# Two decoder layers on one core: the plain up-weight tile split first and kept in a slot, two more landing buffers, six staggered gate tiles ahead of the pairs, a later sample-state update

## The chip, the core and the metric

The kernel runs on one core of one Trainium2 chip. The metric is the device time of one execution in microseconds (us); lower is better. The engines are named as the profile names them: PE (TensorE, matmuls), DVE (VectorE), ACT (ScalarE), POOL (GpSimd), SP (SyncE, which issues the DMAs here). Each engine works through its own list of instructions in order; an instruction that has to wait holds up all that stand behind it on the same engine.

## What is computed

1024 prompt positions and 8 sample positions (together W = 1032 columns) go through two decoder layers with shared weights, width 1024, FFN width 2816:

```python
def swiglu(hn, w_gate_up, w_down):
    gu = hn @ w_gate_up
    return (jax.nn.silu(gu[..., :D_FF]) * gu[..., D_FF:]) @ w_down

def run_trunk(...):
    for layer in range(DEPTH):                      # DEPTH = 2
        hn = rmsnorm(x, norm_mix[layer])
        out = mixer_ab(hn, ...) if layer % 2 == 0 else mixer_c(hn, ...)
        x = x + out                                 # residual after the output projection
        x = x + swiglu(rmsnorm(x, norm_ffn[layer]), w_gate_up[layer], w_down[layer])
    y = rmsnorm(x, norm_final)
```

Layer 0 mixes by a gated DeltaNet (4 heads, each with a 128 x 128 state per sample) and an RG-LRU; layer 1 by sliding-window attention. The outputs are the activations and all states. `co_sample` computes the sample part of the DeltaNet, and its second half writes the new states: for each of the 8 parts of the states an outer product (one matmul of 512 columns) is added to the decayed old state.

## The kernel before

**Numbers in pieces.** Every fp32 weight tile is split into a high part `wh` (cast on ACT) and a low part `wl` (difference on DVE); activations are split the same way. A product is then three matmuls per 128 rows of contraction: wh·xh, wh·xl, wl·xh.

**Gate and up by seven products.** For each of the KF = 22 feature tiles f, gate and up weights (A11, A12 for gate, A21, A22 for up, each half of the contraction) and the two halves of the columns (B11, B21 and B12, B22) are multiplied in Winograd's form of Strassen's scheme. Seven products of 4 x 3 matmul groups stand for eight: A11·B11, A12·B21, S1·T1, S2·T2, S3·T3, S4·B22 and A22·T4. S1 to S4 are sums of weight tiles that POOL makes (`Pair.sums`, four operations); T1 to T4 are sums and differences of activation tiles that `co_blocks` makes on DVE and POOL, in four steps k = 0 to 3, each of which also makes the k-th quarter of T2 and B22; T1, T3 and T4 are split after the four steps. The evacuations of the products (`plus`) are DVE's, those of A11·B11 and A12·B21 ACT's.

**Ahead of the pairs.** T2 needs the normalised activations of both column halves, A11·B11 and A12·B21 only those of the first. So `run_gu` computes these two products of the first AHEAD = 4 tiles before anything else, one tile after the other (`first(f)`, then `second(f, a)`). The second product adds to the bank that ACT has copied out after the first, so it waits for that copy. Then come the pairs: those four tiles with five products each (S2, S1, S3, S4, A22), the other 18 with seven.

**Weights on their way.** SP loads a raw tile of 512 KB into one of two landing buffers (`raw`); it is split into a ring of WB = 4 pairs `wh`, `wl`; a buffer is loaded again when all of its readers are done (`read`, `load_raw`). `split_next` takes the next weight unit of the list `units`; it is called twice after every product, and a unit can be split only when the unit four places before it has been used up. In a pair the unit A22 is last, so the up tile's buffer stays taken until then.

**What sets the order.** The program is written out by a scheduler (`Sched`) with its own cost model: main products are emitted in order, and the generators (`co_blocks`, `co_sample`, `co_h`, ...) are woken between matmuls when the model's clock says that their inputs are ready. What each engine gets is a fixed list. Intermediate tiles live in SLOTS = 40 slots of one buffer, which `alloc` and `halloc` (half a slot) hand out.

**The sample-state update** (second half of `co_sample`) may start when `in1` (the input projection) is done and more than 4 slots are free.

## Time and profile before

| | us |
|---|---|
| median of 3 runs (lowest, highest) | 2420.78 (2417.97, 2423.76) |
| the profiled execution's own time | 2415.7 |
| its span, first to last instruction | 2413.7 |
| PE busy (share of the span) | 2291.8 (95%) |
| DVE, ACT, POOL busy | 1323.1, 990.9, 808.4 |
| mean granted clock of PE | 0.981 of full speed |

The page gives for each engine its busy share in 40 equal slices of 60 us. PE stands at 9 (over 90%) nearly everywhere; the slices that do not are where the FFN of a layer begins: from about 540 to 660 us (the tenth and eleventh slice) for layer 0, and from about 1690 to 1750 us (the 29th) for layer 1. A time in a row of the timeline is counted from the span's start; "[4.77 <-ACT s L235]" means that the engine sat idle for 4.77 us before that row and that ACT, writing a tile s, ended it. All instructions bear the line of the helper that records them (L235), so rows are told apart by engine, tile name and shape: `wh`, `wl` are split weights, `raw` a landing buffer, `s` a slot, `PS` a PSUM bank.

### The profile page before, as it was taken

Reading aid. Unit: us, or ns where it says so; the run is one execution under the profiler, and the core shown is the slowest. Engines: PE = TensorE matmul, PEld = TensorE weight load, DVE = VectorE, ACT = ScalarE, POOL = GpSimd, SP = SyncE. Lnnn points to the kernel's source line nnn. Section 1 sums busy time; section 2 is a strip of 40 time slices with the busy share of each in tenths; the row PEclk is TensorE's granted clock in tenths of the full one; section 3 lists DMA queues with packets and bytes.
Section 4 is the critical chain, followed back from the end, with each engine's and each line's share of the span. In section 5 each row is a group of like instructions: output and inputs, shape, how many; then the busy total and the mean of one; then the engine's idle time right before and its main releaser. Section 6 shows DMA issues by size and latency. Waiting matters only on the chain.

```text
span 2413.7 us, 40193 instructions
## 1 busy us (share of the span) xinstructions
PE 2291.8 (95%) x15984; PEld 2119.8 (88%) x15984; DVE 1323.1 (55%) x2295; ACT 990.9 (41%) x2015; POOL 808.4 (33%) x738
## 2 busy tenths in 40 slices
PE   9899999997699999999999999999799999999998
PEld 6779988786599999999999789778699999999998
DVE  7888586575644444462336557556654444462324
ACT  6676765533222222241214677654322222241214
POOL 1534363243444444410002444432454444420003
PEclk9999999998699999999999999999899999999999
DMA  4342123254122222263213211334122222262312
GB/s 156 105 126 80 40 91 102 77 166 121 49 82 83 81 82 76 79 239 100 102 51 109 77 56 56 128 118 141 53 81 78 80 79 79 80 246 91 99 53 84
DMA packets 114747, 233.90 MB, mean 97 GB/s; under 512 B 23728, under 2 KB 50144, under 8 KB 114528
## 3 DMA queue, kind: packets, MB, share of 16 engines
q1 hardware_dynamic: 114272, 231.05, 29.9%
q8 instruction: 126, 2.06, 0.4%
q14 instruction: 61, 0.50, 0.1%
q10 hardware_dynamic: 288, 0.29, 0.0%
HBM read 187.72 MB, written 45.66 MB: 97 GB/s over the span
## 4 chain that ended last, share of the span: by engine, by line
PE 77%; DVE 10%; ACT 5%; issue 4%; POOL 2%; DMA 1%; SPq 0%; DVEq 0%; ACTq 0%; POOLq 0%
PE PS L235 77%; DVE s L235 7%; ACT s L235 3%; DVE wl L235 2%; POOL s L235 2%; ACT wh L235 1%; DVE oss L235 0%; SPq L235 0%; DMA s<-ckT 0%; ACT L235 0%; DMA raw<-wgu 0%; DMA hd<-s 0%; DMA s<-xT 0%; ACT mx L235 0%; DMA raw<-wout 0%
## 5 line engine op out<-in xcount | busy, mean ns | idle before, releaser
L235 PE MATMUL PS<-s,wh 128*128 128x260 f32 (+3 forms) x8640 | 1724.2, 316 | 69.5 <-ACT s L235 39.7
L235 PEld LDWEIGHTS PS<-s,wh 128*128 128x128 f32 x8640 | 1326.3, 190 | 154.2 <-ACT s L235 51.7
L235 PE MATMUL PS<-s,wl 128*128 128x260 f32 (+3 forms) x4320 | 1045.7, 314 | 0.0
L235 PEld LDWEIGHTS PS<-s,wl 128*128 128x128 f32 x4320 | 714.9, 190 | 33.2 <-issue 0.9
L235 POOL TENSOR_TENSOR s<-s,s 128x520 f32<-128x520 f32 (+6 forms) x214 | 305.7, 1430 | 781.3 <-ACT s L235 702.6
L235 DVE TENSOR_TENSOR wl<-raw,wh 128x512 fp32r<-128x512 f32 (+1 forms) x403 | 342.6, 855 | 382.9 <-ACT wh L235 382.4
L235 DVE TENSOR_TENSOR s<-PS,s 128x520 f32<-128x520 f32 (+7 forms) x430 | 293.5, 683 | 381.7 <-PE PS L235 302.4
L235 ACT CAST wh<-raw 128x512 fp32r<-128x512 f32 (+1 forms) x428 | 257.5, 608 | 385.5 <-PE PS L235 365.8
L235 POOL TENSOR_TENSOR s<-raw 128x512 f32<-128x512 f32 x88 | 115.1, 1308 | 383.6 <-DMA raw<-wgu 383.6
L235 DVE TENSOR_TENSOR wl<-s,wh 128x512 fp32r<-128x512 f32 x176 | 150.3, 855 | 168.8 <-ACT wh L235 148.0
L235 ACT CAST wh<-s 128x512 fp32r<-128x512 f32 x176 | 108.7, 620 | 298.8 <-POOL s L235 220.9
L235 PE MATMUL PS<-s,s 64*64 64x64 f32 (+11 forms) x1936 | 210.0, 288 | 12.8 <-DVE s L235 7.0
L235 PEld LDWEIGHTS PS<-s,s 128*128 128x128 f32 (+3 forms) x1936 | 171.9, 158 | 47.9 <-issue 15.6
L235 ACT ACTIVATE s<-s 128x520 f32<-128x520 f32 (+5 forms) x197 | 123.4, 632 | 194.1 <-DVE s L235 172.6
L235 ACT COPY s<-PS 128x512 f32<-128x512 f32 (+6 forms) x296 | 129.6, 468 | 170.9 <-PE PS L235 162.1
L235 DVE TENSOR_TENSOR s<-s,s 128x520 fp32r<-128x520 f32 (+8 forms) x186 | 168.9, 934 | 40.7 <-ACT s L235 38.7
L235 ACT CAST s<-s 128x520 fp32r<-128x520 f32 (+4 forms) x200 | 138.7, 711 | 103.5 <-DVE s L235 48.2
L235 DVE SCALAR_TENSOR_TENSOR s<-s,smt,s 128x512 f32<-128x512 f32 (+3 forms) x151 | 121.6, 832 | 13.9 <-ACT s L235 13.4
L235 PE MATMUL PS<-con,s 128*128 128x128 f32 (+2 forms) x659 | 91.3, 271 | 26.1 <-ACT s L235 15.5
L235 PEld LDWEIGHTS PS<-con,s 128*128 128x128 f32 (+1 forms) x659 | 77.0, 155 | 37.8 <-ACT s L235 17.0
L235 POOL TENSOR_SCALAR s<-s,mx 128x256 f32<-128x256 f32 x64 | 64.5, 1020 | 108.4 <-ACT s L235 71.8
L235 POOL TENSOR_TENSOR s<-s,con 64x256 f32<-64x256 f32 (+1 forms) x56 | 59.4, 1062 | 64.7 <-ACT s L235 30.2
(176 smaller groups left out, 1038.2 us busy)
## 6 DMA issues: line engine op xcount, KB each, us to landing
raw<-wgu SPq DMA_DIRECT2D x96, 512.0 KB, 3.6
raw<-win SPq DMA_DIRECT2D x47, 512.0 KB, 3.6
s<-hd SPq DMA_DIRECT2D x44, 516.0 KB, 6.0
raw<-wout SPq DMA_DIRECT2D x32, 512.0 KB, 3.5
raw<-wdn SPq DMA_DIRECT2D x24, 512.0 KB, 3.7
raw<-wqkv SPq DMA_DIRECT2D x24, 512.0 KB, 3.5
hd<-s SPq DMA_DIRECT2D x44, 260.0 KB, 4.4
hd<-s SPq DMA_DIRECT2D x44, 256.0 KB, 3.3
```

Source lines behind the costliest of these rows:

```text
L235: return sched.call(eng, op, lambda: f(*a, **kw), a, kw)
```

## The change

1. AHEAD goes from 4 to 6, and the twelve early products are staggered: the first product of tile f+1 stands between the first and the second of tile f. Each early tile's two results share one slot (`twins`).
2. RAW_MORE = 2: when the first column half of the output projection is done, two slots become further landing buffers (`more_raws`); they are given back in the early loop.
3. In each pair the unit A22 is split first, into a slot of its own and outside the ring, so that the sums and this split free the up tile's buffer at once. It asks for three free slots, unless a product already needs it (`force`).
4. The sample-state update waits for `steady` (the fourth pair of layer 0) as well as `in1`, with more than 2 free slots. `co_blocks` takes its sums in pairs of halves.

```diff
-AHEAD = 4
+AHEAD = 6
+RAW_MORE = 2
+    def twins():
+        wait_free()
+        t, i = new_slot(F32)
+        owner[i] = 0
+        return [Buf(t[:, HW * h:HW * (h + 1)], i, h, F32) for h in range(2)]
...
     def read(raw):
         raw.left -= 1
-        while rpos[0] < len(raws) and raws[rpos[0] - 2].left == 0:
+        if raw.left == 0:
+            h = raw.home
+            if isinstance(h, str) or more[0]:
+                homes.append(h)
+            else:
+                free(h)
+        while rpos[0] < len(raws) and homes:
             load_raw()
+    def more_raws(n):
+        more[0] = n
+        if n:
+            homes.extend(alloc() for _ in range(n))
+            while rpos[0] < len(raws) and homes:
+                load_raw()
...
-        if u >= WB and units[u - WB].left and not units[u - WB].keep:
+        x = units[u]
+        r = x.r - x.slot
+        if r >= WB and ring_units[r - WB].left:
             return
...
+        elif x.slot:
+            if len(free_slots) < 3 and not force:
+                return
+            x.buf = alloc(F32R)
...
-            yield have("in1")
-            yield lambda: len(free_slots) > 4
+            yield have("in1", "steady")
+            yield lambda: len(free_slots) > 2
...
-                self.units(("S2", "S1", "S3", "S4", "A22") if f < AHEAD else
-                           ("A11", "S2", "A12", "S1", "S3", "S4", "A22"), layer)
+                self.units(("A22", "S2", "S1", "S3", "S4") if f < AHEAD else
+                           ("A22", "A11", "S2", "A12", "S1", "S3", "S4"), layer)
...
-                for f in range(AHEAD):
-                    a, p = first(f)
-                    kept_[f] = p, second(f, a)
+                pend = None
+                for f in range(AHEAD + 1):
+                    pg = twins() if f < AHEAD else None
+                    new = first(f, pg[0]) + (pg[1],) if f < AHEAD else None
+                    if f:
+                        kept_[f - 1] = pend[1], second(f - 1, pend[0], pend[2])
+                    pend = new
+                    if f == AHEAD - 3:
+                        more_raws(0)
                 for f in range(KF):
+                    if f == 3:
+                        ready.add("steady")
```

How the lists move is shown at three places. SP, start of the FFN of layer 0, before; `raw` is loaded from `wgu`, and `o_pgc` to `o_s_lru` are small outputs:

```order
L235 DMA raw_5789<-wgu 128x1024
L235 DMA o_pgc<-PGC_101 128x36
...
L235 DMA o_s_gdn<-s18_612 128x4x128
L235 DMA s18_612<-s_gdn_in 128x4x128
L235 DMA raw_5866<-wgu 128x1024
L235 DMA raw_5915<-wgu 128x1024
L235 DMA raw_5940<-wgu 128x1024
```

The same place now (`raw0`, `raw1`, `s33`, `s34` are the four landing buffers):

```order
L236 DMA s33_5197<-wgu 128x1024
L236 DMA s16_5085<-xT 128x520
L236 DMA xe06_118<-s2_4993 128x520
L236 DMA s34_5198<-wgu 128x1024
L236 DMA xe07_119<-s16_5085 128x520
L236 DMA o_pgc<-PGC_101 128x36
...
L236 DMA raw1_5823<-wgu 128x1024
L236 DMA raw0_5881<-wgu 128x1024
L236 DMA s33_5197<-wgu 128x1024
```

In the first list raw_5866 and raw_5915 are gate and up of pair 0, right behind four early tiles; in the second the last three rows are early tile 5 and then gate and up of pair 0, with five early tiles ahead of them and no state loads between. DVE, layer 0, before, from the last early split to the middle of step k = 1 of `co_blocks` (the rows with smt are its scaled activations; the row with con is the sample update):

```order
L235 TENSOR_TENSOR wl_5912<-raw_5789,wh_5911 128x512
L235 TENSOR_TENSOR wl_5933<-s17_5934,wh_5932 128x512
L235 TENSOR_TENSOR wl_5958<-s1_5929,wh_5957 128x512
L235 TENSOR_TENSOR wl_5976<-s17_5934,wh_5975 128x512
L235 TENSOR_TENSOR s21_5106<-s15_3580,con_73 128x512
L235 TENSOR_TENSOR wl_5999<-s16_5935,wh_5998 128x512
L235 TENSOR_TENSOR s23_789<-PS_72,s23_789 128x512
L235 SCALAR_TENSOR_TENSOR s6_4364<-s6_4364,smt_74,s37_1537 128x520
L235 SCALAR_TENSOR_TENSOR s9_4900<-s9_4900,smt_74,s37_1537 128x520
```

DVE, layer 0, now, from the splits between steps 0 and 1 to the splits between steps 1 and 2:

```order
L236 TENSOR_TENSOR wl_5878<-raw0_5583,wh_5877 128x512
L236 TENSOR_TENSOR wl_5899<-s34_5198,wh_5898 128x512
L236 TENSOR_TENSOR wl_5920<-s33_5197,wh_5919 128x512
L236 TENSOR_TENSOR wl_5940<-raw1_5823,wh_5939 128x512
L236 SCALAR_TENSOR_TENSOR s7_4324<-s7_4324,smt_74,s12_5801 128x520
L236 SCALAR_TENSOR_TENSOR s11_4868<-s11_4868,smt_74,s12_5801 128x520
...
L236 TENSOR_TENSOR wl_5967<-s34_5198,wh_5966 128x512
L236 TENSOR_TENSOR wl_5987<-raw1_5823,wh_5986 128x512
L236 TENSOR_TENSOR s13_5992<-s33_5197,s13_5992 128x512
L236 TENSOR_TENSOR wl_6017<-s30_5993,wh_6016 128x512
L236 TENSOR_TENSOR wl_6040<-s30_5993,wh_6039 128x512
```

Before, all four splits of S sums (rows wl from an s) stand ahead of step 1; now step 1 stands ahead of them, between early splits, and then come A22 (s13) and two S splits. PE, the sample update's matmul (s with s, 512 columns) before, within the first product of pair 0, S2·T2:

```order
L235 MATMUL PS_72<-s27_5898,wh_5932 128x260 x4
L235 MATMUL PS_72<-s27_5898,wl_5933 128x260 x2
L235 MATMUL PS_72<-s21_5106,s15_3580 128x512
L235 MATMUL PS_72<-s31_6018,wh_5932 128x260 x4
L235 MATMUL PS_72<-s31_6018,wl_5933 128x260 x2
```

PE now, where the first of these matmuls stands, in the product S4·B22 of pair 3:

```order
L236 MATMUL PS_72<-s35_5910,wh_6586 128x260 x4
L236 MATMUL PS_72<-s35_5910,wl_6587 128x260 x2
L236 MATMUL PS_72<-s17_6029,wh_6586 128x260 x3
L236 MATMUL PS_72<-s15_3610 128x512
L236 MATMUL PS_72<-s17_6029,wh_6586 128x260
```

Before, three of the eight stood in the output projection, one in the first early product and four in pair 0; now all eight stand in pairs 3 to 7.

## Rows read from the trace of the kernel before

**Rows 1.** The page's 40 slices: busy tenths of PE in each.

```profile
PE   9899999997699999999999999999799999999998
```

**Rows 2.** Stretches: busy us (and instructions) by engine, granted clock, DMA share, GB/s.

```profile
558.20:650.80 92.60, 58.50 (x248) 46.84 (x247) 56.49 (x69) 26.94 (x49) 35.88 (x34) 0.72 0.24 70
650.80:690.00 39.20, 34.60 (x280) 33.67 (x280) 18.59 (x24) 8.15 (x14) 18.64 (x13) 1.00 0.28 82
1670.50:1739.20 68.70, 49.23 (x243) 40.47 (x242) 45.29 (x55) 25.68 (x47) 30.05 (x30) 0.85 0.20 62
1739.20:1800.00 60.80, 57.22 (x447) 55.27 (x446) 29.03 (x38) 14.75 (x25) 27.18 (x20) 1.00 0.27 88
```

**Rows 3.** Waits of PE from 558.2 to 650.8: total us, times, longest.

```profile
PE PS L235 <- ACT s L235: 21.2, 9, 5.0
PE PS L235 <- DVE s L235: 11.6, 10, 2.4
```

**Rows 4.** Timeline of PE, layer 0: start, us, instruction, [idle before].

```profile
557.83 0.40 PE L235 MATMUL PS<-s,wl 128*128 128x260 f32 x2
...
574.16 0.73 PE L235 MATMUL PS<-s,wh 128*128 128x512 f32 x2 [0.67 <-ACT s L235]
...
591.28 1.22 PE L235 MATMUL PS<-s,wh 128*128 128x512 f32 x2 [4.77 <-ACT s L235]
...
602.54 0.80 PE L235 MATMUL PS<-s,wh 128*128 128x260 f32 x2 [5.03 <-ACT s L235]
...
623.42 0.80 PE L235 MATMUL PS<-s,wh 128*128 128x260 f32 x2 [1.33 <-DVE wl L235]
...
650.35 0.61 PE L235 MATMUL PS<-s,wl 128*128 128x260 f32 x2
```

**Rows 5.** Timeline of SP's queue, layer 0.

```profile
573.28 17.68 SPq L235 DMA_DIRECT2D raw<-wgu  x3
```

**Rows 6.** Timeline of POOL, layer 0: the first sum of pair 0.

```profile
585.08 1.29 POOL L235 TENSOR_TENSOR s<-raw 128x512 f32<-128x512 f32 x1 [6.61 <-DMA raw<-wgu]
```

**Rows 7.** Timeline of ACT, layer 0: the first split of a sum.

```profile
587.75 0.62 ACT L235 CAST wh<-s 128x512 fp32r<-128x512 f32 x1 [7.13 <-POOL s L235]
```

**Rows 8.** Timeline of DVE, layer 0.

```profile
578.79 1.30 DVE L235 TENSOR_TENSOR s<-s,s 128x520 fp32r<-128x520 f32 x2 [0.69 <-ACT s L235]
...
588.40 2.76 DVE L235 TENSOR_TENSOR wl<-s,wh 128x512 fp32r<-128x512 f32 x2 [7.70 <-ACT wh L235]
...
592.78 1.78 DVE L235 TENSOR_TENSOR s<-s,con 128x512 fp32r<-128x512 f32 x1
...
602.52 3.14 DVE L235 TENSOR_TENSOR s<-s,s 128x520 fp32r<-128x520 f32 x2 [0.69 <-ACT s L235]
```

**Rows 9.** Timeline of PE, layer 1.

```profile
1670.17 0.40 PE L235 MATMUL PS<-s,wl 128*128 128x260 f32 x2
...
1672.77 2.29 PE L235 MATMUL PS<-con,s 128*128 128x1 f32 x20
...
1679.03 0.62 PE L235 MATMUL PS<-s,wh 128*128 128x512 f32 x2
...
1679.72 0.62 PE L235 MATMUL PS<-s,wh 128*128 128x512 f32 x2
...
1731.54 0.64 PE L235 MATMUL PS<-s,wh 128*128 128x260 f32 x4
...
1734.41 0.64 PE L235 MATMUL PS<-s,wh 128*128 128x260 f32 x4
...
1738.92 0.40 PE L235 MATMUL PS<-s,wl 128*128 128x260 f32 x2
```

**Rows 10.** Timeline of DVE, layer 1: scaled activations of steps 2 and 3, then six differences.

```profile
1704.88 1.42 DVE L235 SCALAR_TENSOR_TENSOR s<-s,smt,s 128x520 f32<-128x520 f32 x2
...
1712.06 1.42 DVE L235 SCALAR_TENSOR_TENSOR s<-s,smt,s 128x520 f32<-128x520 f32 x2
...
1719.67 5.88 DVE L235 TENSOR_TENSOR s<-s,s 128x520 fp32r<-128x520 f32 x6
```

More of the change, by code (lines that the diff above doesn't have):

```diff
@@ L454, in __init__ @@
         def __init__(self, wap, nk):
-            self.wap, self.nk, self.left, self.tile = wap, nk, 0, None
+            self.wap, self.nk, self.left, self.tile, self.home = wap, nk, 0, None, None
             raws.append(self)
     class Unit:
-        def __init__(self, key, src, n, left, raw=None, keep=False, before=None, after=None):
+        def __init__(self, key, src, n, left, raw=None, keep=False, before=None, after=None, slot=False):
             self.key, self.src, self.n, self.left, self.raw = key, src, n, left, raw
             self.keep, self.before, self.after = keep, before, after
+            self.slot, self.buf, self.r = slot, None, len(ring_units)
+            if not keep and not slot:
+                ring_units.append(self)
             if raw is not None:
@@ L486, in raw_dma @@
         SP.dma_start(out=raws[i].tile[:, a:b], in_=raws[i].wap[:, a:b])
+    homes = ["raw0", "raw1"]
+    more = [0]
     def load_raw(dma=True):
@@ L490, in load_raw @@
         rpos[0] += 1
-        raws[i].tile = ring_tile(wpool, "raw", 2, [128, 8, 128], F32)
+        h = raws[i].home = homes.pop(0)
+        raws[i].tile = ring_tile(wpool, h, 1, [128, 8, 128], F32) if isinstance(h, str) else \
+            h.a[:, 0:1024].rearrange("p (k c) -> p k c", k=8)
         if dma:
@@ L496, in read, with split_next @@
         raw.left -= 1
-        while rpos[0] < len(raws) and raws[rpos[0] - 2].left == 0:
-            load_raw()
-    def split_next():
+        if raw.left == 0:
[5 more added lines that the diff above has]
+        while rpos[0] < len(raws) and homes:
+            load_raw()
+    def more_raws(n):
[4 more added lines that the diff above has]
+                load_raw()
+        else:
+            for h in [h for h in homes if not isinstance(h, str)]:
+                homes.remove(h)
+                free(h)
+    def split_next(force=False):
         u = upos[0]
@@ L512, in split_next @@
             h, l = (kept[-1].a[:, 512 * i:512 * i + 512].rearrange("p (k c) -> p k c", k=4) for i in range(2))
+        elif x.slot:
+            if len(free_slots) < 3 and not force:
+                return
+            x.buf = alloc(F32R)
+            h, l = (x.buf.a[:, 512 * i:512 * i + 512].rearrange("p (k c) -> p k c", k=4) for i in range(2))
         else:
@@ L1514, in co_blocks @@
                 x1a, x2a = half(k, 0), half(4 + k, 0)
-                ls = [halloc() for _ in range(4)]
+                if k % 2 == 0:
+                    l13 = [twins() for _ in range(3)]
+                ls = [l13[0][k % 2], halloc(), l13[1][k % 2], l13[2][k % 2]]
                 l1, l2, l3, l4 = (b.a[:, 0:520] for b in ls)
@@ L1551, in __init__ @@
                     self.g = Raw(wgu[layer, f], 8)
-                    self.units(("A11", "A12"), layer)
                     return
@@ L1566, in units @@
                         raw, o = self.u if name == "A22" else self.g, 0 if name == "A11" else 4
-                        Unit(key, lambda raw=raw, o=o: raw.tile[:, o:o + 4], 4, 1, raw, before=first)
+                        Unit(key, lambda raw=raw, o=o: raw.tile[:, o:o + 4], 4, 1, raw, before=first,
+                             slot=name == "A22")
                     else:
@@ L1589, in ffn @@
             hd = [dpool.tile([128, W], F32, tag=f"hd{layer}{f}", name=f"hd{layer}{f}", bufs=1) for f in range(KF)]
-            for f in range(AHEAD):
-                Pair(layer, f, True)
+            firsts = [Pair(layer, f, True) for f in range(AHEAD)]
+            for f in range(AHEAD + 1):
+                if f < AHEAD:
+                    firsts[f].units(("A11",), layer)
+                if f:
+                    firsts[f - 1].units(("A12",), layer)
             for f in range(KF):
@@ L1616, in product @@
                 unit_of[key].left = 0
+                if unit_of[key].slot:
+                    free(unit_of[key].buf)
                 if f == KF - 1:
@@ L1638, in run_gu, with first @@
                 two = lambda b: split(b.a[:, 0:520], 2)
-                def first(f):
+                def first(f, p=None):
                     a = bank("mm", 2)
                     product(f, "A11", "B11", a, n1, True, False)
-                    p = halloc()
+                    p = p or halloc()
                     A.copy(out=p.a[:, 0:512], in_=a[:, 0])
@@ L1647, in first, with second @@
                     return a, p
-                def second(f, a):
+                def second(f, a, g=None):
                     product(f, "A12", "B21", a, n1, False, True)
-                    g = halloc()
+                    g = g or halloc()
                     A.activation(out=g.a[:, 0:512], in_=a[:, 0], func=AF.Silu)
```

9 lines of the change are left out of this document (6 added, 3 removed).

## The prediction, written before the changed kernel was timed

> **What bounds the kernel now.** I read the page's slices first: PE is over 90% busy almost everywhere, so no engine's total is the limit, only places where PE is held up. Its slices fall to 7 and 6 around 600 us and to 7 around 1720 us [rows 1], the two places where an FFN begins. Next I read busy time by stretch, from the end of each output projection to the end of pair 0 [rows 2]. In layer 0 this takes 92.60 us with PE busy for 58.50 at a granted clock of 0.72; in layer 1 it takes 68.70, busy 49.23, clock 0.85. The reader is to see two losses: idle time (34.1 and 19.5 us), and matmuls that ran partly at 1.2 instead of 2.4 GHz.
>
> What the stretch would take without loss follows from the timeline. A product of 512 columns takes 2.78 us (four k of 0.695), one of twice 260 takes 2.87 (1731.54 to 1734.41) [rows 9]; the norm's small matmuls take 2.3 [rows 9], and I estimate 0.7 for its five transposes. Before, the stretch holds eight early products and five of pair 0: 8 x 2.78 + 5 x 2.87 + 3.0 = 39.6 us. So layer 0 loses 92.6 - 39.6 = 53.0 us and layer 1 68.7 - 39.6 = 29.1.
>
> The waits name the reason. In layer 0 PE waits 21.2 us for ACT and 11.6 for DVE [rows 3]. The longest waits tell how. At 591.28 the second product of the last early tile waits 4.77 us for ACT to copy out its first [rows 4]. That copy stands on ACT behind the split of a sum, which waited 7.13 for POOL [rows 7]; POOL waited 6.61 for pair 0's up tile [rows 6], whose load stood in SP's queue behind the buffers that early tiles held [rows 5]. The same block reaches DVE, 7.70 us before 588.40 [rows 8]. It has the four S splits, and the sample update, ahead of step 1 of the activations. So step 1 comes late, and at 602.54 PE waits 5.03 us for the second quarter of T2 [rows 4]. After that PE runs at the pace of the steps.
>
> **The change part by part.** No product, split or sum is added or dropped; the early tiles are only computed sooner. The four more early products in each layer (two tiles) cost nothing, but they move 4 x 2.78 = 11.1 us of later work into the stretch, where it covers waiting. Two more gate tiles in each layer are loaded twice; SP and the DMA engines have room (DMA share 0.24 and 0.20 in the stretches [rows 2]).
>
> *Length of the new stretch.* With 12 + 5 products and no loss it is 12 x 2.78 + 5 x 2.87 + 3.0 = 50.7 us. What ends it is the DVE list, so I count that, from the output projection's end, with the lists in the section on the change. Step 0 starts at about 11 us: two products and the norm (2.78 + 2.3 + 2.78), transposes 0.7, then an ACT copy of the norm, one of a bank and a cast, each near 0.62 [rows 7], and a split of 0.65. Steps 2 and 3 start 7.18 us apart in layer 1 [rows 10], with one S split of 1.38 between [rows 8], so a step takes 5.8 with its wait for ACT and POOL beside it. Four steps make 23.2. Between the steps stand 12 splits (four early, two early + A22 + two S, two S + A22) of 0.65 to 1.4 [rows 8]; at 0.8 that is 9.6. I put waits inside at 2: the split for S4 needs a ring place that the twelfth early product frees only at 2.3 + 0.7 + 12 x 2.78 = 36.4. Sum: 11 + 23.2 + 9.6 + 2 = 46 us for the last quarter of T2. PE has its early products done at 36.4, three quarters of S2·T2 at 38.6, and then waits some 7 us.
>
> From there to the end of pair 0 DVE must evacuate four products (0.7 each), split four S and make twelve splits of T1, T3, T4. Six differences took 5.88 beside POOL [rows 10], two took 1.30 alone [rows 8]; at 0.8 that is 9.6 + 2.8 + 4 x 0.9 = 16, and the last product's end adds 3. In layer 1 before, the same piece took from 1719.67 [rows 10] to 1739.3 [rows 9], 19.6, part of it at half clock. I take 19. The stretch is then 46 + 19 = 65 us, 14 above the ideal. Its bounds are 56 (every difference at 0.65, step 0 sooner) and 75 (differences at 1.57, as at 602.52 [rows 8], plus half clock after the wait).
>
> *Gain of the stretch.* Layer 0: 92.6 + 11.1 - 65 = 38.7. Layer 1: 68.7 + 11.1 - 65 = 14.8. This holds what staggering removes, the 0.67 us waits of a second product for ACT's copy [rows 4] among them, since a product of 2.78 now stands between; a late copy on ACT is covered up to that length.
>
> *A22 first, more buffers.* Before, an up tile's buffer was free only after the pair's last split, and in pairs 1 to 3 PE still lost 39.2 - 34.6 = 4.6 us in layer 0 and 60.8 - 57.2 = 3.6 in layer 1 [rows 2], waiting for sums. Now the next loads start as soon as the sums are made, a product or more earlier. I take 6 of the 8.2 (bounds 0 and 8.2). In the pairs from 4 on PE stands at 9 and nothing can be won.
>
> *Sample update.* Its DVE rows (up to 1.78 us [rows 8]) leave the layer 0 stretch; that gain is within the 38.7. In pairs 3 to 7 it adds eight matmuls of about 0.25 (a third of 0.695) where PE is full, of which five stood in the stretch with its idle time: -1.3. Each may wait for its DVE row, between 0 and 1.78 - 0.65 = 1.1; I take 0.5, -4 in all. The three that stood in the output projection give back as much each, 1.5. Sum: -3.8, bounds +1 and -9.
>
> *Redraw.* The unit check now counts in order of creation, not of use, and slots are handed out otherwise, so lists inside the mixers change too, without aim. I take 0, bounds -10 and +6.
>
> **Sum:** 38.7 + 14.8 + 6 - 3.8 = 55.7, say 56 us. Of the profiled execution's 2415.7 us that leaves 2359.7, a factor of 0.9768. The median of the runs shown is 5.1 above that execution; the factor on 2420.78 gives 2365.
>
> One rule of the skill speaks against the count. POOL's sums of pair 1 now fall beside steps 2 and 3, and the row at 602.52 shows differences of 1.57 us beside POOL against 0.65 alone [rows 8]. The Trainium skill, GPSIMD Engine Reference, section 8 "Key points", says that GpSimd shares its SBUF interfaces with VectorE and contends with Vector instructions of two SBUF inputs, which all these differences are. The trace agrees with its direction. If it hit each of the 28 differences of steps and T splits, at 0.77 above the 0.8 counted, it would add 21 us in each layer and give 2407; if it hit none, at 0.15 below, the stretch would be 4 shorter.
>
> **Rivals.** *DVE's chain eats the gain.* If half of the 28 differences in steps and T splits cost 1.57, they take 14 x 0.77 = 10 us more, and the stretch is 75: 20 us less gain, 36 in all, 2385. For it: 602.52 and the half clock in both stretches. Against it: six differences at 1719.67 averaged 0.98 with sums beside them [rows 10]. A bad redraw of 20 us ends at the same place.
>
> *Nearly the whole hole closes.* Stretches of 56 give 18 more, 74 us, 2347. For it: most of layer 0's block was one chain (load, sum, split), which goes. Against it: the steps themselves, 23.2 us of DVE, stay.
>
> *Slower: the split queue starves in the pairs.* A22 wants three free slots, and if it doesn't find them no later unit is split either, until a product asks; PE then waits for cast and difference, 1.33 us at 623.42 [rows 4], where S1's split came that late. With two such products in each of 44 pairs this is 117 us, and the kernel ends 60 above before, near 2482; from 21 such pairs on it outweighs the gain. Against it: DVE's new list shows each A22 split four products ahead of its use; the trace can't show the slots.
>
> *The change doesn't do what it says.* Pair 0's up tile is loaded into the buffer of early tile 3, so its load can't start before that tile's last split, about 21 us in; sums then start at about 25, not much sooner than before (585.08 - 558.2 = 26.9 [rows 6]). If DVE blocks behind them all the same, only the 11.1 us of cover in each layer are won: 2399. Against it: step 1 now stands ahead of the S splits.
>
> **Chances.** Forecast 0.60, with a range of its own of 2353 to 2377; DVE's chain or a bad redraw 0.19; only the cover 0.06; the whole hole 0.09; starved splits 0.03; a redraw that eats all, no change, 0.03. A difference of 0.2% (5 us) is about what a measurement can tell. Faster 0.94, same 0.03, slower 0.03. The range is 2345 to 2392: it takes in the whole-hole case and the slow chain and leaves out the last cases.
>
> **What would show it.** By stretch, from each output projection's end to A22·T4 of pair 0: 65 us with 17 products, clock above 0.85. On PE: no wait above 1 us between early products, one of 5 to 8 at the last quarter of S2·T2, some of 1 to 2 in S1·T1, S3·T3 and A22·T4. On POOL: the first sum about 25 us in, without holding up step 1. In pairs 1 to 3 at most 1 us idle in each layer; about 0.5 at each sample matmul. I am wrong if step 1 waits behind the sums, if pairs 4 to 21 show new waits, or if the time before 540 us moves by more than 10.

## The result, and the profile after

The changed kernel takes 2399.52 us in the median (2395.59 to 2400.39, 4 runs) against 2422.16 us for the kernel before in the same comparison (2417.97 to 2423.76, 4 runs): a ratio of 0.9906, 95% interval 0.9888 to 0.9924. That is 22.6 us faster, where 56 were forecast, and outside the range of 2345 to 2392. The profiled execution of the changed kernel took 2400.15 us (span 2398.1).

The slices of PE and of its clock, after (compare [rows 1]): the dips at 600 and 1720 us are still there, and the clock is low in them.

```profile
PE   8999999899699999999999999999799999999998
...
PEclk9999999999799999999999999999899999999999
```

By stretch, after (columns as in [rows 2]; the row 621.80:647.25 is the last piece of the first stretch, from the last quarter of S2·T2 to the end of A22·T4):

```profile
570.06:647.25 77.19, 57.90 (x291) 49.22 (x290) 54.89 (x61) 30.83 (x56) 31.34 (x32) 0.84 0.22 65
647.25:690.00 42.75, 40.05 (x322) 39.49 (x322) 23.61 (x29) 9.55 (x16) 24.86 (x17) 0.98 0.33 108
1661.45:1736.19 74.74, 57.58 (x291) 48.44 (x290) 55.32 (x62) 30.72 (x56) 31.04 (x32) 0.84 0.20 64
1736.19:1800.00 63.81, 59.88 (x494) 59.13 (x493) 33.90 (x42) 14.74 (x25) 40.02 (x28) 1.00 0.28 96
621.80:647.25 25.45, 18.94 (x102) 17.20 (x103) 16.47 (x22) 10.07 (x18) 3.75 (x3) 0.70 0.03 11
```

The stretches take 77.2 and 74.7 us with four products more, where 65 was forecast for each. The first of them starts at 570.06 in place of 558.2: the mixer and the output projection of layer 0 got 11.9 us longer. The longer of PE's waits in the first stretch are now these (compare [rows 4]):

```profile
609.13 0.51 PE L236 MATMUL PS<-s,wh 128*128 128x260 f32 x2 [1.36 <-ACT s L236]
...
621.80 0.80 PE L236 MATMUL PS<-s,wh 128*128 128x260 f32 x2 [10.39 <-ACT s L236]
...
625.89 0.80 PE L236 MATMUL PS<-s,wh 128*128 128x260 f32 x2 [1.38 <-DVE wl L236]
...
642.13 0.51 PE L236 MATMUL PS<-s,s 128*128 128x260 f32 x2 [1.79 <-ACT s L236]
643.62 3.84 PE L236 MATMUL PS<-s,s 128*128 128x260 f32 x16 [0.97 <-DVE s L236]
```

No wait stands among the twelve early products (before, 4.77 and several of 0.67), and one long wait is left, 10.39 at the last quarter of S2·T2 (10.25 in layer 1). POOL's first sum of pair 0 no longer waits for a load (compare [rows 6]) and starts 24.6 us into the stretch, as forecast. DVE and POOL side by side tell why step 3 is late all the same (compare [rows 8]):

```profile
582.91 0.70 DVE L236 TENSOR_TENSOR s<-s,s 128x520 f32<-128x520 f32 x1
...
595.02 3.20 DVE L236 TENSOR_TENSOR s<-s,s 128x520 fp32r<-128x520 f32 x2 [0.69 <-ACT s L236]
598.14 1.78 DVE L236 TENSOR_TENSOR wl<-s,wh 128x512 fp32r<-128x512 f32 x1
599.84 1.78 DVE L236 TENSOR_TENSOR wl<-raw,wh 128x512 fp32r<-128x512 f32 x1
...
612.22 3.41 DVE L236 TENSOR_TENSOR wl<-s,wh 128x512 fp32r<-128x512 f32 x2
```

```profile
594.66 1.30 POOL L236 TENSOR_TENSOR s<-s 128x512 f32<-128x512 f32 x1
...
597.62 3.46 POOL L236 TENSOR_TENSOR s<-raw,s 128x512 f32<-128x512 f32 x2
...
613.38 5.08 POOL L236 TENSOR_TENSOR s<-s,s 128x512 f32<-128x512 f32 x3
```

A row of two inputs from SBUF takes 0.70 on DVE alone and 1.4 to 1.8 while POOL runs such a row of its own; POOL's go from 1.30 to 1.7. Thirteen DVE rows of layer 0's stretch are slow in this way, twelve of them ahead of the last quarter of T2. Eight meet the two groups of sums; the other five meet differences of activations that POOL makes for `co_blocks`, right behind each group of sums and in step 3.

To compare kernels without the mixers I use the time from the first early product to the first matmul of the down projection, summed over the two layers, and call it the stage time. Before and after it is 503.35 + 478.53 = 981.9 and 481.19 + 471.30 = 952.5 us:

```profile
558.07:1061.42 503.35, 463.02 (x3200) 430.23 (x3199) 247.43 (x320) 144.76 (x250) 208.93 (x173) 0.95 0.28 87
1670.41:2148.94 478.53, 453.88 (x3196) 423.76 (x3195) 235.94 (x305) 143.88 (x248) 202.89 (x169) 0.98 0.27 86
```

```profile
570.06:1051.25 481.19, 454.64 (x3204) 427.45 (x3202) 264.51 (x324) 145.81 (x252) 216.38 (x178) 0.97 0.30 96
1661.45:2132.75 471.30, 449.25 (x3196) 422.41 (x3194) 243.76 (x309) 145.99 (x252) 203.69 (x170) 0.97 0.26 89
```

It comes from one execution each. Two pairs of kernels below have nearly the same lists in these stages; they differ by 0.2 us (after and e1) and 2.3 us (e3 and e5). A third pair, before and e13, has the same lists in layer 1 and differs there by 1.0 us; in layer 0, where e13 has four DVE rows and one matmul of the sample update less, it differs by 4.7. So a difference of 3 to 6 us counts only where the timeline shows its place.

### The profile page after: what moved, and what is told of

The parts are those of the page before. It is cut to its first block, busy times and chain, and to the rows that moved or that the text cites. A ratio compares the mean times of both kernels' runs of the same rounds, so it can differ in the third digit from the quotient of the medians.

```text
span 2398.1 us, 40100 instructions
## 1 busy us (share of the span) xinstructions
PE 2289.8 (95%) x15984; PEld 2124.7 (89%) x15984; DVE 1343.4 (56%) x2295; ACT 989.3 (41%) x2014; POOL 817.1 (34%) x738
## 4 chain that ended last, share of the span: by engine, by line
PE 64%; DVE 3%; ACT 1%; issue 1%; POOL 1%; SPq 0%; DMA 0%; DVEq 0%; ACTq 0%; POOLq 0%
PE PS L236 64%; DVE s L236 2%; ACT s L236 1%; DVE wl L236 1%; POOL s L236 1%; SPq L236 0%; DMA s<-ckT 0%; ACT wh L236 0%; DVE mx L236 0%; ACT mx L236 0%; DVEq L2430 0%; POOL n L236 0%; DVEq L236 0%; DVE PN L236 0%; ACTq L236 0%
## 5 line engine op out<-in xcount | busy, mean ns | idle before, releaser
L236 PE MATMUL PS<-s,wh 128*128 128x260 f32 (+4 forms) x7936 | 1606.1, 318 | 53.8 <-ACT s L236 30.5
L236 PEld LDWEIGHTS PS<-s,wh 128*128 128x128 f32 x7936 | 1231.5, 190 | 131.6 <-ACT s L236 36.5
L236 PE MATMUL PS<-s,wl 128*128 128x260 f32 (+4 forms) x3968 | 977.1, 317 | 0.0
L236 PEld LDWEIGHTS PS<-s,wl 128*128 128x128 f32 x3968 | 659.0, 190 | 33.4 <-issue 0.9
L236 DVE TENSOR_TENSOR wl<-raw,wh 128x512 fp32r<-128x512 f32 (+1 forms) x335 | 275.1, 826 | 312.1 <-ACT wh L236 309.5
L236 ACT CAST wh<-raw 128x512 fp32r<-128x512 f32 x360 | 216.4, 608 | 394.6 <-PE PS L236 370.7
L236 PE MATMUL PS<-s,s 128*128 128x260 f32 (+12 forms) x2944 | 344.0, 289 | 8.7 <-ACT s L236 4.5
L236 PEld LDWEIGHTS PS<-s,s 128*128 128x128 f32 (+3 forms) x2944 | 302.9, 171 | 44.0 <-issue 17.0
L236 DVE TENSOR_TENSOR s<-s,s 128x520 fp32r<-128x520 f32 (+7 forms) x188 | 169.9, 928 | 48.2 <-ACT s L236 46.4
L236 PE MATMUL PS<-con,s 128*128 128x128 f32 (+2 forms) x659 | 93.1, 273 | 30.8 <-DVE s L236 14.3
L236 PEld LDWEIGHTS PS<-con,s 128*128 128x128 f32 (+1 forms) x659 | 77.9, 157 | 42.6 <-DVE s L236 15.6
L236 POOL TENSOR_TENSOR s<-raw 128x512 f32<-128x512 f32 x42 | 56.4, 1342 | 86.3 <-DMA hd<-s 66.3
```

The lines of the kernel that those rows point to most:

```text
L236: return sched.call(eng, op, lambda: f(*a, **kw), a, kw)
```

## The experiments

All ratios are to the kernel before, run beside them. The runs were timed in several sessions, so the ratio compares two of them better than the median.

| run | median us | ratio (95%) | stage time us |
|---|---|---|---|
| before | | 1 | 981.9 |
| after | 2399.5 | 0.9906 (0.9888–0.9924) | 952.5 |
| e1 ring | 2392.2 | 0.9884 (0.9859–0.9908) | 952.7 |
| e2 DVE sums | 2401.2 | 0.9917 (0.9885–0.9949) | 946.3 |
| e3 pair order | 2385.2 | 0.9859 (0.9841–0.9877) | 938.2 |
| e4 sample early | 2403.2 | 0.9942 (0.9922–0.9962) | 951.6 |
| e5 ring + order | 2378.6 | 0.9813 (0.9798–0.9827) | 940.5 |
| e6 e1 + fill | 2389.1 | 0.9866 (0.9849–0.9883) | 950.7 |
| e7 e1, two buffers | 2423.3 | 1.0001 (0.9987–1.0016) | 986.1 |
| e8 e1, A22 last | 2390.8 | 0.9860 (0.9843–0.9877) | 949.5 |
| e9 before + buffers | 2412.9 | 0.9958 (0.9941–0.9974) | 969.5 |
| e10 e1, unstaggered | 2405.0 | 0.9928 (0.9902–0.9954) | 965.3 |
| e11 e5, pair 1 held | 2368.3 | 0.9784 (0.9746–0.9823) | 934.5 |
| e12 e5, A22 last in 0, 1 | 2374.1 | 0.9804 (0.9768–0.9840) | 936.5 |
| e13 before + redraw | 2430.1 | 1.0034 (1.0018–1.0049) | 976.2 |
| e14 e11, pair 0 on DVE | 2364.8 | 0.9766 (0.9735–0.9797) | 930.6 |
| e15 e5, both held | 2368.4 | 0.9789 (0.9759–0.9819) | 932.6 |

**The redrawn lists (e1, e13).** e1, on the changed kernel:

```diff
             units[u + 1], units[u + 2] = units[u + 2], units[u + 1]
+            x, y = units[u + 1], units[u + 2]
+            ring_units[x.r], ring_units[y.r] = y, x
+            x.r, y.r = y.r, x.r
```

> The changed kernel with one bookkeeping edit: where the second and third weight unit of a mixer are swapped, their numbers in the ring check are swapped too, so the check counts in order of use again. PE's list up to the output projection of layer 0 is then that of the kernel before. Theory 'redraw': the 11.9 us that the output projection of layer 0 ends later (570.1 against 558.2 us) come from the redrawn lists inside that mixer, so it ends at 558 to 560 again, the half-clock intervals in the first 500 us go from 31 us back to about 10, and the kernel takes 2387 to 2390 us, 10 to 12 less than the changed one. Rival 'loads': the two further landing buffers or the clock by chance make the mixer late; then it still ends near 570 and the time stays within 3 us of 2399.5.

e13, on the kernel before:

```diff
-        if u >= WB and units[u - WB].left and not units[u - WB].keep:
+        if x.r >= WB and ring_units[x.r - WB].left:
             return
```

> The kernel before with nothing but the changed ring check (a place in the ring is counted in order of creation, not of use). Its PE list up to the output projection of layer 0 is that of the changed kernel, what follows is that of the kernel before. Theory 'redraw': the first 560 us get 7 to 14 us longer and the kernel takes 2428 to 2436 us. Rival 'together': the mixer is late only with the further buffers' loads beside it, and the time stays within 4 us of before (2418 to 2425 us).

With e1 the output projection ends at 554.12 in place of 570.06, and the stage time does not move; by medians the gain is 7.3 us, with intervals that overlap. The lists up to there are the same in after, e2 and e3, which reach this point at 565.3 to 572.7, and the same in e1 and seven other runs with its edit (e5, e6, e8, e11, e12, e14, e15), which reach it at 553.7 to 560.1: the two groups don't overlap. e13 settles it: the redraw alone makes the kernel before 0.34% slower (0.18 to 0.49), 8.2 us, and its output projection ends at 573.47. The rows are the time to that point, for before, e13 and e1:

```profile
0.00:558.20 558.20, 524.73 (x3931) 464.69 (x3932) 415.20 (x844) 340.88 (x690) 216.13 (x242) 0.99 0.35 107
```

```profile
0.00:573.47 573.47, 531.23 (x3932) 469.91 (x3932) 424.60 (x848) 341.17 (x690) 222.63 (x242) 0.98 0.34 105
```

```profile
0.00:554.12 554.12, 524.15 (x3928) 464.69 (x3928) 407.37 (x840) 342.01 (x691) 210.71 (x238) 0.99 0.34 106
```

With as many matmuls PE is busy 6.5 us longer in e13 than before, at a granted clock of 0.98 against 0.99, and idle 8.8 us longer. These 15.3 us are more than the kernel loses by its medians, as part of the sample update moves ahead of the stage, which gets 5.7 us shorter. "Together" falls.

**Contention (e2, e11, e12, e14, e15).** e2, with the three other sums changed alike (e14 has `< 1` in place of `< 2`, on top of e11):

```diff
+                E = V if self.f < 2 else G
-                G.tensor_tensor(out=s1, in0=a21, in1=a22, op=ALU.add)
+                E.tensor_tensor(out=s1, in0=a21, in1=a22, op=ALU.add)
...
```

> The changed kernel with the four sums of pair 0 and of pair 1 made by DVE in place of POOL, in each layer. Theory 'contention': DVE's two-input rows take 1.6 to 1.8 us while POOL makes these sums (13 such rows in layer 0) and 0.65 alone; with the sums on DVE they take 0.65 to 0.7, which saves 13 x 1.0 = 13 us of DVE per layer, and 8 more rows of 0.65 cost 5.2. Each stretch gets about 7 us shorter (layer 0: 77.2 to 70, layer 1: 74.7 to 68), the kernel 2383 to 2388 us. Rival 'number of rows': DVE's list is long as it stands and its rows are slow for another reason; they stay at 1.6 in the steps, 8 rows of 1.6 come on top, each stretch is 5 to 13 us longer, and the kernel takes 2410 to 2425 us.

DVE after step 1 in e2:

```profile
599.24 2.11 DVE L236 TENSOR_TENSOR s<-s,s 128x520 fp32r<-128x520 f32 x2 [0.69 <-ACT s L236]
601.27 0.68 DVE L236 TENSOR_TENSOR wl<-s,wh 128x512 fp32r<-128x512 f32 x1
601.88 0.68 DVE L236 TENSOR_TENSOR wl<-raw,wh 128x512 fp32r<-128x512 f32 x1
602.48 1.79 DVE L236 TENSOR_TENSOR s<-s 128x512 f32<-128x512 f32 x1
```

The same splits take 0.68 in place of 1.78: their slowness comes from POOL's sums. The last quarter of S2·T2 starts 49.7 and 49.8 us into the stretches (51.7 and 53.4 in the changed kernel). The size was missed: the stage time falls by 6.2 us, not 14. The eight sums cost DVE 7.2 us in layer 0, not 5.2, and only eight of the thirteen slow rows met weight sums; a row that meets one of POOL's differences is slow still, such as the sum at 602.48. The median doesn't show the gain (this mixer ended at 572.72). e11 only holds the A22 split of pair 1, and with it the sums of pair 1, back, on e5:

```diff
+            if x.key[1] == 1 and ("T2", 3) not in xb and not force:
+                return
             if len(free_slots) < 3 and not force:
                 return
```

> The kernel of the fifth experiment (ring check and order of products) with pair 1's A22 split, and with it pair 1's four sums on POOL, held back until step 3 of the activations is through. Theory 'contention': six or seven DVE rows of steps 2 and 3 and the splits between them take 0.65 to 0.7 again instead of 1.6 to 1.8, the last quarter of S2T2 starts 5 to 7 us sooner, some of the splits of T1 and T3 get slow instead, and each stretch is 3 to 5 us shorter: 2368 to 2373 us. Rival 'conserved': the sums collide with the splits of T3 and T1 as they did with the steps, and the stretches stay at 77 us: 2376 to 2381 us.

The last quarter of S2·T2 starts 600.83 - 553.85 = 47.0 us into the stretch (52.0 in e5) and waits 5.54 in place of 10.34. A wait of 3.10 is new: it stands in S3·T3, the next product in this order, for the low part of T3's first quarter, whose DVE rows now run beside the sums:

```profile
600.83 0.80 PE L236 MATMUL PS<-s,wh 128*128 128x260 f32 x2 [5.54 <-ACT s L236]
...
609.02 0.80 PE L236 MATMUL PS<-s,wh 128*128 128x260 f32 x2 [3.10 <-DVE s L236]
```

The stage time is 6.0 us shorter than e5's, the median 10 (the intervals overlap): the sums collide with fewer rows that PE waits for, but they still collide. e14 and e15 were to tell whether the place of the sums matters; e15 has this line in place of e11's:

```diff
+            if (x.key[1] == 0 and ("T2", 2) not in xb or x.key[1] == 1 and ("T1", 3) not in xb) and not force:
+                return
```

> The eleventh experiment's kernel (pair 1 held back until step 3 is through) with pair 0's four sums on DVE in place of POOL. Theory 'contention': the six rows of 1.6 to 1.8 us in and behind step 1 fall to 0.65 (6 us less), the sums add 4 x 0.65 = 2.6 and perhaps one wait for the load; the last quarter of S2T2 starts 2 to 4 us sooner and the kernel takes 2360 to 2366 us. Rival 'it is the number of rows': 0 to 3 us more, 2368 to 2372 us.

> The fifth experiment's kernel with both pairs' sums held back: pair 0's until step 2 of the activations is through, pair 1's until T1 is split. Theory 'contention': steps 1 and 2 run undisturbed (12 us apart becomes 9), but pair 0's sums and splits then stand between step 2 and step 3 and S2T2 starts late; both together about as the eleventh experiment, 2364 to 2373 us. Rival 'sums first': PE waits for S2's split with nothing else to do, 5 to 10 us longer in each layer than the eleventh, 2378 to 2388 us.

e14 takes another 3.9 us off the stage time; the last quarter comes 45.1 us into the stretch of layer 0 and 46.6 into that of layer 1, 1.9 sooner than in e11 in both. It has the lowest ratio of the study, 0.9766, though its interval overlaps those of e11 and e15. e15 stands 2 us from it in stage time, within what two executions differ by. e12 gets pair 1's sums out of the way in another way:

```diff
-                self.units(("A22", "S2", "S3", "S1", "S4") if f < AHEAD else
+                self.units(("S2", "S3", "S1", "S4", "A22") if f < 2 else
+                           ("A22", "S2", "S3", "S1", "S4") if f < AHEAD else
```

> The kernel of the fifth experiment with A22 split last in pairs 0 and 1 alone, first in all others. In the eighth experiment A22 last in all pairs made the stretches 4.8 and 5.5 us shorter and the pairs behind them in layer 0 7.4 us longer. Theory 'A22 first pulls pair 1's sums into the steps': the stretches are 4 to 6 us shorter and the other pairs unchanged: 2367 to 2371 us. Rival: the price of A22 last is paid in pairs 1 and 2 themselves (A22T4 waits 2 us or more for its split), and the time is 2374 to 2380 us.

It gains 4.0 us of stage time and 4.5 in the median (overlapping), at the edge of the second theory. Both hold in part: the stretches are 4.5 and 6.8 us shorter than in e5, the pairs behind them 5.3 and 2.0 longer.

**Order of products (e3, e5).** The pairs behind the stretch, after:

```profile
652.08 0.75 PE L236 MATMUL PS<-s,wh 128*128 128x260 f32 x4 [0.86 <-DVE s L236]
...
667.67 0.72 PE L236 MATMUL PS<-s,wh 128*128 128x260 f32 x4 [0.95 <-DVE s L236]
...
683.14 0.72 PE L236 MATMUL PS<-s,wh 128*128 128x260 f32 x4 [0.88 <-DVE s L236]
```

e3 exchanges S1 and S3 in the units, T1 and T3 in `co_blocks`, and the products in `run_gu`; e5 is e3 with e1's edit.

```diff
-                self.units(("A22", "S2", "S1", "S3", "S4") if f < AHEAD else
+                self.units(("A22", "S2", "S3", "S1", "S4") if f < AHEAD else
...
+                    d = bank("mm", 2)
+                    if early:
+                        product(f, "S3", "T3", d, n2, True, False)
+                        after()
                     product(f, "S1", "T1", b, n2, False, True)
```

> The changed kernel with another order of products in the six pairs whose gate tile is early: S2T2, S3T3, S1T1, S4B22, A22T4 in place of S2T2, S1T1, S3T3, S4B22, A22T4, and the splits in the same order. Theory 'bank': the 0.9 us that PE waits once in each of these pairs (652.08, 667.67, 683.14, ...) is S1T1, which adds to a bank that DVE must first have read after S2T2; with S3T3 between, the wait goes in pairs 1 to 5 of each layer, 10 x 0.9 = 9 us, and the kernel takes 2389 to 2392 us. Theory 'sums' (as the prediction had it): PE waits there for the sums of the next pair, the order of products changes nothing, and the time stays within 3 us of 2399.5.

> Both edits that helped: the ring check counted in order of use (first experiment) and the order S2T2, S3T3, S1T1, S4B22, A22T4 in the pairs with an early gate tile (third). If redraw and bank waits are separate causes, their gains add up: the profiled kernel with the first edit took 2384.6 us and the order took 12.7 us off the pairs of both layers, so 2372 to 2380 us in the median. If they share a cause (the lists drawn anew by either), the time stays near 2385 to 2392 us.

These waits are gone: from 642.26 to 740 e3 has one wait left, of 0.48 us at another product:

```profile
713.66 3.16 PE L236 MATMUL PS<-s,s 128*128 128x260 f32 x24 [0.48 <-DVE s L236]
```

The stage time falls by 14.3 us in e3 and 12.2 in e5 against e1; the ten waits at S1·T1 of pairs 1 to 5 took 10.7 in the changed kernel, and what made the rest isn't shown. So PE waited there for DVE to read the bank of S2·T2 before S1·T1 adds to it, not for sums. The edits of e1 and e3 add up: e5's median lies 6.6 below e3's and 13.6 below e1's, and its ratio below both.

**Landing buffers, staggering, A22 first (e7 to e10).** The lines of e7, e8 and e10, each on e1; e9 is the kernel before (AHEAD = 4, plain early loop, A22 last in the ring, sample update early) with RAW_MORE = 2; it is cut down from the changed kernel, so it keeps the shared slots of the early results and the sums in pairs of halves.

```diff
-RAW_MORE = 2
+RAW_MORE = 0
```

```diff
-                self.units(("A22", "S2", "S1", "S3", "S4") if f < AHEAD else
-                           ("A22", "A11", "S2", "A12", "S1", "S3", "S4"), layer)
+                self.units(("S2", "S1", "S3", "S4", "A22") if f < AHEAD else
+                           ("A11", "S2", "A12", "S1", "S3", "S4", "A22"), layer)
```

```diff
+                for f in range(AHEAD):
+                    pg = twins()
+                    a, p = first(f, pg[0])
+                    kept_[f] = p, second(f, a, pg[1])
```

> The kernel of the first experiment without the two further landing buffers (RAW_MORE = 0). Theory 'buffers matter': the early tiles are loaded into two buffers only, so early splits wait for loads, and PE waits between early products as it did before (4 to 8 us), pair 0's sums come later than 25 us into the stretch, and each stretch gets 4 to 10 us longer: 2400 to 2412 us. Rival 'buffers idle': the ring of eight splits holds the loads back in any case, and the slow part is DVE's list; the stretches stay at 77 and 74 us, the time within 4 us of 2392.

> The kernel before with only the two further landing buffers of the change (four early tiles, not staggered, A22 split last and in the ring, sample update early, ring check in order of use). Theory 'the buffers carry the gain': without them the rest of the change was worth nothing (2423.3 us), so alone they bring most of it: pair 0's up tile is loaded 15 us or more earlier, step 1 no longer waits behind the sums, and the time is 2390 to 2402 us. Rival 'only together': with four early tiles PE runs out of work, DVE's list of steps is as long as it was, and the time is 2412 to 2424 us.

> The kernel of the first experiment (changed kernel, ring check in order of use) with the twelve early products in pairs, A11 and A12 of a tile behind each other, in place of staggered. Theory of the prediction, 'staggering covers ACT's copy': each tile's second product waits 0.67 us or more for the copy of its first, or the split behind it, 6 per layer: 8 us longer, near 2400. Rival 'DVE sets the end': PE waits at the last quarter of S2T2 some 10 us in any case, so waits between early products are taken out of that one: the time stays within 4 us of 2392.

> The kernel of the first experiment with A22 split last in each pair again (still into its own slot and outside the ring). Theory of the prediction, 'A22 first frees the buffer': the next pair's loads start later again, PE waits twice per pair instead of once in pairs 1 to 5 (0.9 us each), and maybe more in the stretch, so 8 to 12 us longer, 2400 to 2405 us. Rival 'no effect in the pairs': the waits there are the bank's (0.9 us once in a pair) with either order, and the sums of pair 1 come later in the stretch, so fewer of DVE's rows fall beside POOL's: the stretches are 2 to 5 us shorter, 2385 to 2392 us.

Without the two buffers the whole gain is gone. Its queue of loads, POOL's first sum and DVE's step 0:

```profile
566.04 44.87 SPq L236 DMA_DIRECT2D raw<-wgu  x9
```

```profile
591.49 1.29 POOL L236 TENSOR_TENSOR s<-raw 128x512 f32<-128x512 f32 x1 [24.33 <-DMA raw<-wgu]
```

```profile
595.17 3.39 DVE L236 TENSOR_TENSOR wl<-s,wh 128x512 fp32r<-128x512 f32 x3 [1.84 <-ACT wh L236]
598.49 0.75 DVE L236 SCALAR_TENSOR_TENSOR s<-s,smt,s 128x520 f32<-128x520 f32 x1
```

Step 0 now stands behind S splits, as step 1 did in the kernel before, 38.4 us into the stretch (580.78 - 570.06 = 10.7 in the changed kernel). Alone the buffers bring 12.4 us of stage time (e9), nearly all in layer 0; everything else without them brings nothing (e7 is 4.2 us longer than before), together 29.2: they need each other. e9's time, 2412.9, lies in the range of "only together", at its lower end: it is clear of no gain at all (0.9941 to 0.9974), and far from "the buffers carry the gain". Staggering is worth 12.6 us of stage time, since without it PE waits for ACT's copies, and longer the later they come:

```profile
587.09 1.00 PE L236 MATMUL PS<-s,wh 128*128 128x512 f32 x2 [3.02 <-ACT s L236]
...
600.29 1.22 PE L236 MATMUL PS<-s,wh 128*128 128x512 f32 x2 [5.81 <-ACT s L236]
```

A22 last (e8) is no slower: its stretches are 4.8 and 5.5 us shorter, since pair 1's sums come later (first sum 47.0 us into layer 0's stretch, 38.7 in the changed kernel), and layer 0's pairs 7.4 us longer, with A22·T4 waiting for DVE. The first row is the last quarter of S2·T2, the second such an A22·T4:

```profile
604.58 0.80 PE L236 MATMUL PS<-s,wh 128*128 128x260 f32 x2 [5.39 <-ACT s L236]
...
696.80 4.64 PE L236 MATMUL PS<-s,s 128*128 128x260 f32 x24 [3.52 <-DVE s L236]
```

**Sample update (e4) and the clock (e6).** e4, on the changed kernel:

```diff
-            yield have("in1", "steady")
+            yield have("in1")
...
-            if len(free_slots) < 3 and not force:
+            if len(free_slots) < 5 and not force:
```

> The changed kernel with the sample update back where it was (it waits for in1 alone, and its eight matmuls stand in the output projection, the early products and pair 0); so that slots suffice, A22 is split only with five free slots in place of three. Theory 'the move was worth its price' (the prediction: about 4 us lost in the pairs, its gain within the stretch's): its 16 DVE rows, at 0.65 to 1.7 us, come back into DVE's list of the stretch of layer 0, which is 5 to 12 us longer, and the pairs 3 to 7 give back 4 to 6 us; the kernel takes 2399 to 2408 us. Rival 'the move costs': the stretch does not change, the stalls at 699 to 719 us go, and the kernel takes 2392 to 2396 us.

Layer 0's stretch stays at 77.3 us, and the pairs behind it are 3.3 us shorter (400.7 against 404.0); in layer 1, which has no sample update, the pairs are 2.0 us longer, and the stage time of both layers is the same within the noise. The run doesn't show the move alone: by asking for five free slots it also puts off pair 1's sums, from 38.7 to 54.2 us into layer 0's stretch, behind step 3, as e11 does on purpose:

```profile
627.88 1.72 POOL L236 TENSOR_TENSOR s<-raw 128x512 f32<-128x512 f32 x1
```

No run here separates what the sample update's rows add to the stretch from what the later sums take off it.

e6 runs idle matmuls in the long wait, on e1:

```diff
+                    if (f, name, k) == (0, "S2", 3):
+                        for j in range(12):
...
+                                    nc.tensor.matmul(out=PS[:, 2 + c, 0:260], lhsT=wt[:, j % 3, :], rhs=x[:, 260 * c:260 * c + 260],
```

> The kernel of the first experiment (ring check in order of use) with 72 additional matmuls of 128x260 in each layer, whose results nobody reads, ahead of the last quarter of S2T2 in pair 0, where PE waits 10.4 and 10.0 us for step 3 of the activations. They need nothing new and take some 8.6 us; no list of another engine changes. Theory 'clock': this wait is what lowers the clock to 0.5 for the 20.5 us behind it; with PE busy the clock stays at 1.0, the piece from the last quarter to the end of pair 0 falls from 25.5 to 19 to 21 us in layer 0 and from 21.1 to 16 to 18 in layer 1, and the kernel takes 8 to 11 us less than the first experiment's (2381 to 2384 us). Rival 'DVE': that piece goes at DVE's pace (splits and differences), and the clock costs nothing there: it stays at 25 and 21 us and the time within 3 us of 2392. Rival 'clock by budget': the clock falls all the same, or later and longer, since PE has worked more: no gain or a loss of up to 10 us.

The wait is filled, but the last piece still takes 25.1 us and its clock is 0.77 (25.5 us and 0.70 in e1 and in the changed kernel):

```profile
605.60:630.69 25.09, 18.30 (x102) 16.76 (x103) 16.27 (x22) 10.13 (x18) 3.56 (x3) 0.77 0.03 12
```

The clock falls twice within this piece even so, around waits of this piece itself (0.97 and 1.58 us, then 1.77 and 0.98), so the run doesn't separate the two: what the half clock costs there stays open; I estimate between 0 and the 6.1 us by which 18.3 us busy exceed the 0.7 + 4 x 2.87 = 12.2 of full speed. "This wait alone lowers the clock" falls.

## Why the prediction was wrong

The direction was right and the size was not. By its terms, in the profiled executions:

| term | forecast | measured |
|---|---|---|
| stretch, layer 0 | 38.7 | 92.6 + 11.1 - 77.2 = 26.5 |
| stretch, layer 1 | 14.8 | 68.7 + 11.1 - 74.7 = 5.1 |
| A22 first and sample update, behind the stretches | 6 - 5.3 = 0.7 | (410.6 - 404.0) + (409.7 - 396.6) - 22.2 = -2.5 |
| redraw and the rest (1.5 of the sample update) | 1.5 | -13.5; the redraw alone 8.2 by e13 |

The sum of the measured column is 15.6, the difference of the two spans; the medians give 22.6, as the profiled execution of before was one of its faster and that of after one of its slower. Of the 40 us that the spans fall short of the forecast, the first piece of the stretches takes 13.1, their second piece 8.8, the pairs 3.2, and the rest, the mixers above all, 15.0.

*Stretch, first piece: failed on the rule it had weighed.* 46 us were forecast to the last quarter of S2·T2; it took 51.7 and 53.4 (1714.85 - 1661.45). Step 0 came at 10.7 as forecast (11). The step that failed is "at 0.8 that is 9.6" and the steps of 5.8: the price of a DVE row beside POOL, 1.57, stood in [rows 8] and was not put in, because six rows of layer 1 "averaged 0.98 with sums beside them" [rows 10]. That average was misread. POOL ran beside the first and the last of the six alone, and these two took 1.74 and 1.77; the four between share the other 2.4 us:

```profile
1719.67 1.74 DVE L235 TENSOR_TENSOR s<-s,s 128x520 fp32r<-128x520 f32 x1
...
1723.77 1.77 DVE L235 TENSOR_TENSOR s<-s,s 128x520 fp32r<-128x520 f32 x1
```

```profile
1719.19 1.67 POOL L235 TENSOR_TENSOR s<-s,s 128x520 fp32r<-128x520 f32 x1 [2.67 <-ACT s L235]
1723.12 1.86 POOL L235 TENSOR_TENSOR s<-raw 128x512 f32<-128x512 f32 x1 [2.27 <-DMA raw<-wgu]
```

With pair 1's sums held back the piece takes 47.0 us in layer 0 (e11; 52.0 in e5), with pair 0's on DVE too 45.1 (e14). That is the 46 of the forecast, so the count of rows seems right and their price wrong. The rule cited, that GpSimd contends with Vector instructions of two SBUF inputs (the Trainium skill, GPSIMD Engine Reference, section 8 "Key points"), is what e2 shows, with 1.78 against 0.68.

*Stretch, second piece: too short, cause partly open.* Forecast 19, measured 25.5 and 21.3. PE was busy 18.9 us at a clock of 0.70 in layer 0. Its waits for DVE and ACT remain when the long wait is filled (e6). Which share DVE's rows and which the clock has in it stays open.

So the rival "DVE's chain eats the gain" (stretch 75) describes the stretches, though they alone, with nothing else amiss, would have left 2385; the redraw came on top. The median of 2399.5 is the number of another rival, only the cover (2399), and that is chance: its condition, DVE blocked behind the sums, didn't come about, as step 1 starts at 591.49 and the first sum at 594.66.

*Redraw: 0 taken, bounds -10 and +6.* It cost 8.2 (e13), within the bounds, though the time to the output projection moved by 11.9, more than the 10 us that the prediction named as a sign of error. The term was put at nothing without a reason, for the lists of a whole mixer in which PE has waits of up to 5.9 us.

*Pairs 1 to 3: +6 taken, wrong mechanism.* "Waiting for sums" was read into 4.6 and 3.6 us of idle time [rows 2]. Of these 8.2 us, 5.1 are six waits of 0.8 to 0.9 at S1·T1. e3 shows that such a wait is that of a bank read before it is added to. One stands in each pair that has no A11 and A12 product between, so two more early tiles bring two more such pairs per layer, and A22 first doesn't touch them. The other 3.1 us are waits at A22·T4 of pairs 1 and 2, in layer 0 these:

```profile
664.49 0.72 PE L235 MATMUL PS<-s,wh 128*128 128x260 f32 x4 [0.96 <-DVE s L235]
...
681.31 0.72 PE L235 MATMUL PS<-s,wh 128*128 128x260 f32 x4 [1.07 <-DVE s L235]
```

They are gone in the changed kernel; which of its parts removed them no run separates. Putting A22 first cost the stretches 5 us each (e8) and repaid it behind them in layer 0 alone.

*Sample update:* -5.3 forecast in the pairs; e4's pairs of layer 0 give back 3.3, with another edit beside it. Whether its leaving shortens the stretch stays open, as e4 put off pair 1's sums as well.

*Staggering and the buffers* were right in kind. The forecast gave the buffers no term of their own; e7 shows that the order "step 1 ahead of the S splits" hangs on them: without them even step 0 stands behind these splits.

## What to carry to other kernels

When work is brought forward, list what then runs at the same time on the other vector engine, and price the rows of both at the slow figure that the trace already shows; an average over rows with and without a neighbour hides it. A short wait that recurs once per tile is best looked up by the instruction that it holds and by what that instruction overwrites; here an exchange of two products took 14.3 us off the stages, where the whole change took 29.4. Compare stages apart, since a bookkeeping edit in a list scheduler can move a stage that the change never meant to touch.

## What the runs showed of the hardware

DVE and POOL go in step when both read two SBUF inputs: one row each per 1.7 us (in the changed kernel POOL's rows start at 597.62, 599.33, 601.04 and DVE's at 598.14, 599.84, 601.55), where they take 0.65 to 0.70 and 1.30 alone, so little less than one after the other (1.95). A DVE row that reads PSUM and one SBUF tile is not slowed: in e11 it takes 0.69 within a POOL sum, and a split 1.7 us later takes 1.75. The Trainium skill, SBUF — State Buffer, section "Who interferes with whom", has this rule, that a DVE instruction with at most one SBUF input, outside the modes that use two ports, does not contend with GpSimd; the trace agrees.

```profile
603.84 0.69 DVE L236 TENSOR_TENSOR s<-PS,s 128x520 f32<-128x520 f32 x1
...
605.52 1.75 DVE L236 TENSOR_TENSOR wl<-s,wh 128x512 fp32r<-128x512 f32 x1
```

```profile
603.33 1.72 POOL L236 TENSOR_TENSOR s<-s,raw 128x512 f32<-128x512 f32 x1
605.01 5.11 POOL L236 TENSOR_TENSOR s<-s,s 128x512 f32<-128x512 f32 x3
```
